# Mean squares by quarters of the tokens, and the root spread by a product, in a two-layer diffusion backbone

## The chip, the cores and the metric

The kernel runs on one core of a Trainium2 chip. The core has a matmul engine (TensorE, called PE in the profile; its loads of the stationary operand are shown apart as PEld), a vector engine (VectorE, DVE), a scalar engine with activation functions (ScalarE, ACT), a general engine (GpSimd, POOL) and a queue that issues transfers (SyncE, SP). Each engine works through its own instructions in order and waits on semaphores for the others. Matmuls write to PSUM, from where DVE and ACT read; everything else lies in SBUF, which has 128 partitions.

The metric is the device time of one execution in microseconds. It is given as the median of several runs. One further execution is profiled, and the rows quoted below are of that one.

## The reference, cut to what matters

There are 512 latent tokens and 256 context tokens of width 1024, all in f32. Layer 0 is grouped-query attention with a norm on every query and key head, layer 1 a bidirectional Mamba-2 mixer; each is followed by a gated FFN with a short convolution. Every one of these four sub-layers begins with an RMS norm over the 1024 features and an adaptive shift and scale:

```python
def rms_norm(x, g):
    xf = x.astype(jnp.float32)
    y = xf * lax.rsqrt(jnp.mean(xf * xf, axis=-1, keepdims=True) + EPS)
    return (y * g.astype(jnp.float32)).astype(x.dtype)

def modulate(x, shift, scale):
    return x * (1 + scale) + shift
...
    q_l = rms_norm(q_l.reshape(bsz, seq, N_HEADS, HEAD_DIM), q_norm)
    k_l = rms_norm(k_l.reshape(bsz, seq, N_KV_HEADS, HEAD_DIM), k_norm)
...
        y = rms_norm(y.reshape(bsz, length, D_INNER) * jax.nn.silu(z), norm_w) @ w_out
```

The norms are the subject here. The first kind takes the mean over 1024 features; the second, of queries and keys, over the 64 features of each head; the third, at the end of the Mamba mixer, over 2048.

## The kernel before

Activations lie transposed: features on the 128 partitions, tokens along the free axis, in eight tiles of 128 features. Weights are split into a high and a low part (`split`: ACT makes the high part, DVE or POOL the low part), and each product is three matmuls (`mm3`, the lines L105, L106 and L108 of the profile).

Since a token's features are spread over partitions, its sum of squares is a sum over partitions, and that is made on PE. `rstd_rows` does it for all norms. The squares are first added up over feature tiles, so one tile `sq` of 128 partitions by n tokens is left. Then:

1. For each 128 tokens a matmul has that piece of `sq` as stationary operand and a column of ones (for the heads: two columns, `g.blk`, one for each head of 64 features) as moving operand. The result (tile `ss...`, L236) has tokens on partitions and one or two columns.
2. DVE and ACT work the inverse root out on this small tile (128x2, 128x4 or 128x12; L239, L241, L243, L244): mean plus epsilon, logarithm, exponential of minus one half, one step of Newton's method. The last operation (L247) writes it out wide: 128 tokens by 128 equal columns (tile `rb...`).
3. After a pause PE transposes each wide piece (L253, tile `rsT...`), so that each of the 128 partitions holds the root for every token. For the segments of the sub-layer norms ACT copies the result to SBUF (`rs...`, L345).

The norms in the program: the first one over 512 latent tokens and one over the context (in `attention`, with the tiles named `a`); ten of query and key pairs (`normed`, named `q`, 768 tokens and two heads each); eight segments of 256 tokens in `Norm.gen` (named `f` for the FFNs, `s` for the Mamba mixer); and one over 512 tokens at the end of the mixer (named `y`). In `Norm.gen` the steps are spread over the steps of the product before, `lag` of them apart, and `modulated` then makes the input of the next product: DVE multiplies (L281), ACT adds the shift, DVE or POOL makes the low part.

The attention loop has eight pairs of heads with seven steps each. A step computes scores (`ps_s`), ACT takes the exponential (`pr`, L676), PE multiplies by the values (`ps_o`), DVE adds the sums (`acc`), and in between PE and DVE find the maxima for the next pair (`ps_m`, `ma`, `mb`). Behind each step `Fill.run` takes other work from a queue: the projections of later pairs (`ps_q`), their norms, products of the conditioning vector (`ps_ada`, transposed by `ps_adt`), later the output projection (`ps_d`). A generator in this queue that yields BREAK is left alone for three steps and costs the step's budget 1.0. The old head norm yields it three times: after the sums, and after each of two groups of transposes (512 and 256 tokens). The order within an engine is set by the program order with priorities by a scheduler when the program is built; the first part of attention is kept in written order.

In the profile some of these tiles carry the engine's read tile behind the arrow: `ssq<-cst,qsq` is the sum over heads, with the constants (`cst`) as moving and the squares (`qsq`) as stationary operand.

Of the kernel before, what the change touches and what calls it, by code (L numbers as in the profile page):

```python
# [7 lines left out]
P = 128  # L8
# [49 lines left out]
CST_IDENT, CST_BLK, CST_SEL, CST_COS, CST_SIN = 0, 128, 130, 132, 132 + L  # L58
NCST = 132 + 2 * L
# [167 lines left out]
def rstd_rows(g, sq, n, cols, width, name, bank):  # L227

    nc = g.nc
    c = cols.shape[-1]
    nt = n // P
    ps = bank(f"ss{name}")
    for t in range(nt):
        nc.tensor.matmul(ps[:, t * c : (t + 1) * c], sq[:, t * P : (t + 1) * P], cols, start=True, stop=True)  # L236
    small = lambda nm: g.p.tile([P, nt * c], F32, tag="rst", bufs=8, name=nm)
    a, y, u = small("rsa"), small("rsy"), small("rsu")
    nc.vector.tensor_scalar(a, ps[:, : nt * c], 1.0 / width, EPS, ALU.mult, ALU.add)  # L239
# [5 lines left out]
    rb = t3(g, f"rb{name}", n=n)  # L245
    wide = lambda v: v.unsqueeze(2).broadcast_to([P, nt * c, P // c])
    nc.vector.scalar_tensor_tensor(rb.rearrange("p (a b) -> p a b", b=P // c), wide(u), 1.5, wide(y), ALU.add, ALU.mult)  # L247
    yield BREAK
    out = []
    for t0 in range(0, nt, 4):  # L250
        pt = bank(f"rsT{name}")
        for t in range(t0, min(nt, t0 + 4)):
            nc.tensor.transpose(pt[:, (t - t0) * P : (t - t0 + 1) * P], rb[:, t * P : (t + 1) * P], g.ident)  # L253
        yield (pt, t0 * P, min(n, (t0 + 4) * P))
# [55 lines left out]
class Norm:  # L310
# [23 lines left out]
    def gen(self, seg, x, lag=2):  # L334

        i, a, b = seg
        g, nc, n = self.g, self.g.nc, b - a
# [7 lines left out]
        nc.scalar.copy(rs, next(rows)[0][:, :n])  # L345
# [33 lines left out]
def attention(g, fill, X, late):  # L379
# [41 lines left out]
    nc.sync.dma_start(g.cst, I["cst"][:, :CST_COS])  # L421
# [9 lines left out]
    def warmth(n):  # L431
        for _ in range(n):
            nc.tensor.matmul(warm[:, :P], g.ones, g.ones, start=True, stop=True)
# [8 lines left out]
    norm = rstd_rows(g, acc, L, g.ones[:, :1], D, "a", Bk)  # L442
# [12 lines left out]
    rsl, _, _ = next(norm)  # L455
# [12 lines left out]
    for m in range(KT):  # L468
# [11 lines left out]
        if m == 3:  # L480
            norm = rstd_rows(g, sqc, C, g.ones[:, :1], D, "a", Bk)
            next(norm)
        if m == 4:
            rsc = t3(g, "rsc", n=C)
            pt, _, _ = next(norm)
            nc.scalar.copy(rsc, pt[:, :C])
# [15 lines left out]
    man.__exit__(None, None, None)  # L502
    nc.sync.dma_start(g.cs, I["cst"][:, CST_COS:])
# [21 lines left out]
    def normed(qs, gain, eng):  # L525
# [51 lines left out]
    onesr = g.const.tile([P, P], F32R, name="onesr")  # L577
    nc.scalar.copy(onesr, g.ones)
# [5 lines left out]
    class Pair:  # L584
# [43 lines left out]
        def steps(self):  # L628
# [10 lines left out]
            def final(po, ps, acc, out):  # L639

                n = out.shape[-1]
                for e in range(2):
                    nc.tensor.matmul(ps[S64[e], :n], g.ones[:, :HD], acc[:, n * e : n * e + n], start=True, stop=True)
# [22 lines left out]
            for t in range(7):  # L666
                ps, pr = Sb("ps_s"), g.t3p.tile([P, 1024], F32, tag="pr", bufs=3, name="pr")
                for q0, n, k0, off in (((0, L, t * P, 0),) if t < 6 else ((L, C, L, 0), (L, C, L + P, C))):
# [5 lines left out]
                    for e in range(2):  # L674
                        nc.tensor.matmul(outs[e], onesr[S64[e]], self.diag[S64[e], q], start=False, stop=True)  # L675
# [203 lines left out]
def ssd(g, x, norm, wf, bg, close):  # L879
# [340 lines left out]
    norm = rstd_rows(g, acc[0], L, g.ones[:, :1], 2 * D, "y", lambda nm: Bank(g, nm))  # L1220
# [225 lines left out]
```

## Time and profile before

| | |
|---|---|
| median of 3 runs | 1912.97 us (1905.94 to 1915.4) |
| profiled execution | 1914.7 us, span of its instructions 1912.9 us |
| mean granted clock of PE | 0.994 |
| PE busy | 1876.5 us |
| DVE busy | 1311.2 us |
| ACT busy | 823.0 us |
| POOL busy | 309.8 us |

A row of a group names line, engine, operation, output and inputs, shape and count; then the busy time in all and the mean duration of one in ns; then the engine's idle time just before, with what ended it. Durations of matmuls overlap, since they are pipelined: what one occupies on PE is read from its start to the start of the next. A row of the time line gives start, duration, engine, line and tiles, and in brackets the idle time before.

### The profile page before, as it was taken

What the parts mean: (1) busy time and instruction counts of PE and PEld (TensorE: products, weight loads), DVE (VectorE), ACT (ScalarE), POOL (GpSimd) and SP (SyncE); (2) the same over time, 40 slices, a digit from 0 to 9 for tenths busy, and PEclk for the clock granted to TensorE, in tenths of its full rate; (3) what the DMA queues carried; (4) which work ended last, traced back from release to release, by engine and by line L of the source; (5) the groups of instructions that cost most, each with busy time, mean ns of one, the idle gap of its engine ahead of it and who ended that gap; (6) DMA issues with size and microseconds to landing.
All of it is one profiled execution on the core that took longest, in us unless ns stands there. A gap on an engine that the chain in (4) does not pass through costs nothing.

```text
span 1912.9 us, 27512 instructions
## 1 busy us (share of the span) xinstructions
PE 1876.5 (98%) x10834; PEld 1547.6 (81%) x10834; DVE 1311.2 (69%) x1943; ACT 823.0 (43%) x1426; POOL 309.8 (16%) x274
## 2 busy tenths in 40 slices
PE   9999999999999999999999999999999999999999
PEld 7866555678888888888888888888888878888887
DVE  5578778678877777444488777777888466565555
ACT  3634444255122222222266777776667352323331
POOL 2241111031000000000040344443434210000000
PEclk9989998999999999999999999999999999999999
DMA  9221332114434555221122443334443322323232
GB/s 337 78 89 45 113 112 95 34 45 166 132 122 132 174 188 166 66 67 60 62 89 87 121 118 115 126 113 133 120 138 115 91 77 86 102 88 110 88 100 88
DMA packets 73425, 210.02 MB, mean 110 GB/s; under 512 B 8912, under 2 KB 14416, under 8 KB 73168
## 3 DMA queue, kind: packets, MB, share of 16 engines
q1 hardware_dynamic: 73296, 208.26, 34.3%
q8 instruction: 85, 1.39, 0.3%
q14 instruction: 44, 0.36, 0.1%
HBM read 198.79 MB, written 6.82 MB: 107 GB/s over the span
## 4 chain that ended last, share of the span: by engine, by line
PE 79%; DVE 9%; issue 3%; ACT 2%; POOL 1%; DMA 1%; DVEq 0%; SPq 0%; POOLq 0%; ACTq 0%
PE ps_up L106 10%; PE ps_up L108 10%; PE ps_up L105 10%; PE ps_d L105 6%; PE ps_d L106 6%; PE ps_d L108 6%; PE ps_in L106 4%; PE ps_in L108 4%; PE ps_in L105 4%; PE ps_o L637 2%; PE ps_s L673 2%; PE ps_st L1033 2%; DVE ht L281 1%; PE ps_wo L108 1%; PE ps_wo L105 1%
## 5 line engine op out<-in xcount | busy, mean ns | idle before, releaser
L87 DVE TENSOR_TENSOR wl<-wst,wh 128x1024 fp32r<-128x1024 f32 x205 | 254.5, 1242 | 244.9 <-PE ps_up L106 137.7
L85 ACT CAST wh<-wst 128x1024 fp32r<-128x1024 f32 x211 | 221.2, 1049 | 423.2 <-DMA wst<-in_wup 333.8
L106 PE MATMUL ps_up<-hlf,wh 128*128 128x512 f32 x1008 | 357.0, 354 | 0.0
L105 PE MATMUL ps_up<-hhf,wh 128*128 128x512 f32 x1008 | 356.9, 354 | 0.0
L108 PE MATMUL ps_up<-hhf,wl 128*128 128x512 f32 x1008 | 356.8, 354 | 0.0
L105 PEld LDWEIGHTS ps_up<-hhf,wh 128*128 128x128 f32 x1008 | 190.5, 189 | 26.5
L106 PEld LDWEIGHTS ps_up<-hlf,wh 128*128 128x128 f32 x1008 | 190.6, 189 | 26.4
L108 PEld LDWEIGHTS ps_up<-hhf,wl 128*128 128x128 f32 x1008 | 190.5, 189 | 26.4
L105 PE MATMUL ps_in<-hhs,wh 128*128 128x512 f32 (+1 forms) x560 | 204.4, 365 | 0.0
L106 PE MATMUL ps_in<-hls,wh 128*128 128x512 f32 (+1 forms) x560 | 199.4, 356 | 0.0
L108 PE MATMUL ps_in<-hhs,wl 128*128 128x512 f32 (+1 forms) x560 | 198.7, 355 | 0.0
L105 PE MATMUL ps_d<-hdh,wh 128*128 128x512 f32 (+1 forms) x568 | 193.6, 343 | 1.4 <-DVE X L784 1.2
L108 PE MATMUL ps_d<-hdh,wl 128*128 128x512 f32 (+1 forms) x568 | 193.5, 341 | 0.0
L106 PE MATMUL ps_d<-hdl,wh 128*128 128x512 f32 (+1 forms) x568 | 193.0, 340 | 0.3 <-DVE hdl L87 0.3
L784 DVE SCALAR_TENSOR_TENSOR X<-ps_d,mod,X 128x512 f32<-128x512 f32 (+1 forms) x224 | 124.6, 583 | 36.9 <-PE ps_d L108 36.6
L106 PEld LDWEIGHTS ps_d<-hdl,wh 128*128 128x128 f32 x568 | 106.6, 188 | 14.8 <-DVE hdl L87 0.7
L105 PEld LDWEIGHTS ps_d<-hdh,wh 128*128 128x128 f32 x568 | 106.3, 188 | 14.8 <-DVE X L784 1.4
L105 PEld LDWEIGHTS ps_in<-hhs,wh 128*128 128x128 f32 x560 | 105.9, 189 | 15.1 <-issue 1.2
L108 PEld LDWEIGHTS ps_in<-hhs,wl 128*128 128x128 f32 x560 | 105.8, 189 | 14.8
L108 PEld LDWEIGHTS ps_d<-hdh,wl 128*128 128x128 f32 x568 | 106.7, 188 | 13.1
L106 PEld LDWEIGHTS ps_in<-hls,wh 128*128 128x128 f32 x560 | 106.0, 189 | 13.2
L676 ACT ACTIVATE pr<-ps_s 128x1024 f32<-128x1024 f32 x56 | 57.2, 1021 | 110.6 <-PE ps_s L675 109.6
(340 smaller groups left out, 3547.3 us busy)
## 6 DMA issues: line engine op xcount, KB each, us to landing
wst<-in_wup SPq DMA_DIRECT2D x88, 512.0 KB, 3.6
wada<-in_adaT SPq DMA_DIRECT2D x56, 512.0 KB, 3.9
wst<-in_win SPq DMA_DIRECT2D x48, 512.0 KB, 3.7
wst<-in_wdown SPq DMA_DIRECT2D x44, 512.0 KB, 3.6
E<-ad SPq DMA_DIRECT2D x64, 256.0 KB, 6.8
wada<-in_adaB SPq DMA_DIRECT2D x24, 512.0 KB, 4.6
ec<-ead SPq DMA_DIRECT2D x64, 128.0 KB, 5.0
wst<-in_wout SPq DMA_DIRECT2D x16, 512.0 KB, 3.6
```

Of the source, the lines that this page charges most:

```text
L85: keep(nc.scalar.copy(hi, src))
L87: keep(eng.tensor_tensor(lo, src, _r(hi), ALU.subtract))
L105: mm(out, wh, ah, start=first, stop=False)
L106: mm(out, wh, al, start=False, stop=False)
L108: mm(out, wl, ah, start=False, stop=last)
L281: nc.vector.scalar_tensor_tensor(t[:, c0:c1], ap, g.moda[layer][ca][:, m, v : v + 1], rs[:, c0:c1], ALU.mult, ALU.mult)
L637: nc.tensor.matmul(po[S64[e], :n], v, pr[:, 512 * e + off : 512 * e + off + n], start=first, stop=last)
L673: nc.tensor.matmul(outs[e], a[S64[e], k], b[S64[e], q], start=i == 0, stop=False)
L676: nc.scalar.activation(pr, ps, AF.Exp)
L784: nc.vector.scalar_tensor_tensor(ap, o[:, c0:c1], gate[:, m, v : v + 1], ap, ALU.mult, ALU.add)
L1033: nc.tensor.matmul(ps[:, d * 256 : (d + 1) * 256], Bt[:, t * P : (t + 1) * P], xw[d][t], start=t == ts[0], stop=t == ts[-1])
```

## The change

The sub-layer norm over a segment of 256 tokens (`rstd_all`) becomes one matmul with ones as the stationary operand and the squares as the moving one, 256 columns. Its result already has the sum on every partition, so nothing is transposed and nothing copied: the five operations of the root run on 128x256.

The norm over 512 tokens (`rstd_quarters`) takes four matmuls, one for each quarter of 128 tokens, with a stationary operand of 32 columns, so that each quarter's sums stand on 32 partitions of PSUM of their own (`sums_by_group`). The root is worked out on 128x128. Four products with a column of the identity, read 128 times, then bring each quarter to all partitions.

The head norm (`rstd_heads`) does the same with quarters of 192 tokens: within the 32 partitions 16 belong to each head. Four products with a pattern (`g.pick`), each over 64 partitions, spread the root; the two row halves write to two PSUM banks. DVE then multiplies twice 384 tokens, not 512 and 256. The generator yields BREAK twice, not three times.

The tile of ones is one column that is read with stride zero, also where scores take up the maxima (`onesr`) and where sums of exponentials are made. The constants grow by `blk` (32 columns) and `pick` (256 columns); they are loaded by a second transfer behind the first part of attention.

```diff
+def rsqrt_mean(g, ps, width, name):
     nc = g.nc
-    small = lambda nm: g.p.tile([P, nt * c], F32, tag="rst", bufs=8, name=nm)
-    a, y, u = small("rsa"), small("rsy"), small("rsu")
-    nc.vector.tensor_scalar(a, ps[:, : nt * c], 1.0 / width, EPS, ALU.mult, ALU.add)
+    n = ps.shape[-1]
+    w = t3(g, f"rs{name}", n=3 * n)
+    a, y, u = (w[:, i * n : (i + 1) * n] for i in range(3))
+    nc.vector.tensor_scalar(a, ps, 1.0 / width, EPS, ALU.mult, ALU.add)
     for f in ((lambda: nc.scalar.activation(y, a, AF.Ln)), (lambda: nc.scalar.activation(y, y, AF.Exp, scale=-0.5))):
         follow(g, f()) if g.tables else f()
     nc.vector.tensor_tensor(u, y, a, ALU.mult)
     nc.vector.scalar_tensor_tensor(u, y, -0.5, u, ALU.mult, ALU.mult)
-    rb = t3(g, f"rb{name}", n=n)
-    wide = lambda v: v.unsqueeze(2).broadcast_to([P, nt * c, P // c])
-    nc.vector.scalar_tensor_tensor(rb.rearrange("p (a b) -> p a b", b=P // c), wide(u), 1.5, wide(y), ALU.add, ALU.mult)
+    nc.vector.scalar_tensor_tensor(a, u, 1.5, y, ALU.add, ALU.mult)
+    return a
+
+def rstd_all(g, sq, width, name):
+    n = sq.shape[-1]
+    ps = Bank(g, f"ss{name}")[:, :n]
+    g.nc.tensor.matmul(ps, g.ones(P), sq, start=True, stop=True)
+    return rsqrt_mean(g, ps, width, name)
+
+def sums_by_group(g, sq, cols, name):
+    n = sq.shape[-1] // 4
+    ps = Bank(g, f"ss{name}")[:, :n]
+    for j in range(4):
+        g.nc.tensor.matmul(ps[32 * j : 32 * j + 32], cols, sq[:, j * n : (j + 1) * n], start=True, stop=True)
+    return ps
+
+def rstd_quarters(g, sq, width, name):
+    n = sq.shape[-1] // 4
+    r = rsqrt_mean(g, sums_by_group(g, sq, g.ones(32), name), width, name)
     yield BREAK
-    for t0 in range(0, nt, 4):
-        pt = bank(f"rsT{name}")
-        for t in range(t0, min(nt, t0 + 4)):
-            nc.tensor.transpose(pt[:, (t - t0) * P : (t - t0 + 1) * P], rb[:, t * P : (t + 1) * P], g.ident)
-        yield (pt, t0 * P, min(n, (t0 + 4) * P))
+    pt = Bank(g, f"rsT{name}")
+    for j in range(4):
+        g.nc.tensor.matmul(pt[:, j * n : (j + 1) * n], g.ident[:, 32 * j : 32 * j + 1].broadcast_to([P, P]), r,
+                           start=True, stop=True)
+    yield pt
+
+def rstd_heads(g, sq, name):
+    n = T // 4
+    r = rsqrt_mean(g, sums_by_group(g, sq, g.blk, name), HD, name)
+    yield BREAK
+    pt = [Bank(g, f"rsT{name}") for _ in range(2)]
+    for i in range(2):
+        for e in range(2):
+            rows = slice(64 * e, 64 * e + 64)
+            g.nc.tensor.matmul(pt[e][:, i * n : (i + 1) * n], g.pick[rows, i * P : (i + 1) * P], r[rows],
+                               start=True, stop=True)
+    yield [(pt[e], 2 * e * n, 2 * e * n + 2 * n) for e in range(2)]
...
-        for r in rstd_rows(g, sq, T, g.blk, HD, "q", Bk):
-            if r is not BREAK:
-                pt, c0, c1 = r
-                nc.vector.tensor_tensor(qs[:, c0:c1], qs[:, c0:c1], pt[:, : c1 - c0], ALU.mult)
-            yield BREAK
+        rows = rstd_heads(g, sq, "q")
+        yield next(rows)
+        for pt, c0, c1 in next(rows):
+            nc.vector.tensor_tensor(qs[:, c0:c1], qs[:, c0:c1], pt[:, : c1 - c0], ALU.mult)
+        yield BREAK
...
-        rows = rstd_rows(g, self.acc[seg, 6], n, g.ones[:, :1], D, self.name, lambda nm: Bank(g, nm))
-        next(rows)
+        rs = rstd_all(g, self.acc[seg, 6], D, self.name)
         for _ in range(lag):
             yield
-        rs = t3(g, f"rs{self.name}", n=n)
-        nc.scalar.copy(rs, next(rows)[0][:, :n])
```

Where instructions move, the built programs show it. PE in pair 0 of the attention loop, third step, before (each row: line, operation, output, moving and stationary tile, output shape, how many in a row):

```order
L236 MATMUL ssq<-cst,qsq 128x2 x6
L673 MATMUL ps_s<-qh,kh_967 128x512 x2
L673 MATMUL ps_s<-qh,kl_968 128x512 x2
L673 MATMUL ps_s<-ql,kh_967 128x512 x2
L675 MATMUL ps_s<-diag_1203,onesr 128x512 x2
L601 MATMUL ps_m<-kh_967,qh 128x256 x4
L637 MATMUL ps_o<-pr,v_744 64x512 x2
L253 MATMUL rsTq<-cst,rbq 128x128 x4
```

and the same place after:

```order
L259 MATMUL ssq<-qsq,cst 32x192 x4
L700 MATMUL ps_s<-qh,kh_912 128x512 x2
L700 MATMUL ps_s<-qh,kl_913 128x512 x2
L700 MATMUL ps_s<-ql,kh_912 128x512 x2
L702 MATMUL ps_s<-diag_1171,onesr 128x512 x2
L628 MATMUL ps_m<-kh_912,qh 128x256 x4
L664 MATMUL ps_o<-pr,v_733 64x512 x2
L286 MATMUL rsTq<-rsq,cst 128x192 x4
```

Six sums of two columns became four of 192 columns on 32 partitions each, and four transposes (two more follow a few steps later) became four products of 192 columns.

PE in pair 5, before, second step, with filling from the queue behind `ps_o`:

```order
L637 MATMUL ps_o<-pr,v_742 64x512 x2
L128 MATMUL ps_ada<-wada,sc_83 32x512 x8
L673 MATMUL ps_s<-qh,kh_1988 128x512 x2
L673 MATMUL ps_s<-qh,kl_1989 128x512 x2
L673 MATMUL ps_s<-ql,kh_1988 128x512 x2
L675 MATMUL ps_s<-diag_2673,onesr 128x512 x2
L601 MATMUL ps_m<-kh_1994,qh 128x512 x2
L637 MATMUL ps_o<-pr,v_743 64x512 x2
L236 MATMUL ssq<-cst,qsq 128x2 x6
```

and a later step of pair 5 after, where the queue has nothing left:

```order
L664 MATMUL ps_o<-pr,v_733 64x512 x2
L700 MATMUL ps_s<-qh,kh_1814 128x512 x2
L700 MATMUL ps_s<-qh,kl_1815 128x512 x2
L700 MATMUL ps_s<-ql,kh_1814 128x512 x2
L702 MATMUL ps_s<-diag_2667,onesr 128x512 x2
L664 MATMUL ps_o<-pr,v_734 64x512
L628 MATMUL ps_m<-kh_1820,qh 128x512 x2
L664 MATMUL ps_o<-pr,v_734 64x512
```

The three `ps_ada` products of pair 5 and its `ssq` stand in pair 4 now, and between the products of scores and values nothing stands in the last four steps.

DVE at the end of attention, the norm of the second segment of 256 tokens, before:

```order
L239 TENSOR_SCALAR rsa<-ssf_4110 128x2
L784 SCALAR_TENSOR_TENSOR X<-ps_d_4123,mod_88,X 128x256
L243 TENSOR_TENSOR rsu<-rsy,rsa 128x2
L244 SCALAR_TENSOR_TENSOR rsu<-rsy,rsu 128x2
L784 SCALAR_TENSOR_TENSOR X<-ps_d_4137,mod_88,X 128x256
L247 SCALAR_TENSOR_TENSOR rbf_4121<-rsu,rsy 128x256
L281 SCALAR_TENSOR_TENSOR ht<-X,moda_99,rsf_4151 128x256
```

and after:

```order
L234 TENSOR_SCALAR rsf_4022<-ssf_4020 128x256
L811 SCALAR_TENSOR_TENSOR X<-ps_d_4043,mod_88,X 128x256
L238 TENSOR_TENSOR rsf_4022<-rsf_4022 128x256
L811 SCALAR_TENSOR_TENSOR X<-ps_d_4061,mod_88,X 128x256
L239 SCALAR_TENSOR_TENSOR rsf_4022<-rsf_4022 128x256
L240 SCALAR_TENSOR_TENSOR rsf_4022<-rsf_4022 128x256
L811 SCALAR_TENSOR_TENSOR X<-ps_d_4080,mod_88,X 128x256
L88 TENSOR_TENSOR wl<-wst,wh 128x1024
L315 SCALAR_TENSOR_TENSOR ht<-X,moda_99,rsf_4022 128x256 x3
```

All four operations of the root are 256 columns wide now, one more eviction (`X<-ps_d`) and a weight split stand ahead of the first modulation, and no wait for PE's transposes lies between.

More of the change, by code (lines that the diff above doesn't have):

```diff
@@ L432, in warmth @@
         for _ in range(n):
[L433 removed]
+            nc.tensor.matmul(warm[:, :P], g.ones(P), g.ones(P), start=True, stop=True)
     warmth(38)
@@ L454, in attention @@
     warmth(5)
-    rsl, _, _ = next(norm)
+    rsl = next(norm)
     next(mods[0])
@@ L480, in attention @@
         if m == 3:
[L481 to L486, printed above, removed]
+            rsc = rstd_all(g, sqc, D, "a")
         for j in range(6):
```

47 lines of the change are left out of this document (23 added, 24 removed).

## The prediction

> **What bounds the kernel now.** I read the page's busy shares and clock row first, then the waits of PE, then the time line around the norms.
>
> ```profile
> PE 1876.5 (98%) x10834; PEld 1547.6 (81%) x10834; DVE 1311.2 (69%) x1943; ACT 823.0 (43%) x1426; POOL 309.8 (16%) x274
> PEclk9989998999999999999999999999999999999999
> DMA  9221332114434555221122443334443322323232
> ...
> PE rsTq L253 <- DVE rbq L247: 2.9, 2, 1.8
> PE rsTs L253 <- DVE rbs L247: 1.3, 2, 1.0
> PE rsTf L253 <- DVE rbf L247: 1.2, 2, 1.0
> ```
>
> PE is busy in 98% of the span and idle for 36.4 us. So the time is PE's work, plus its waits, plus what a lowered clock adds. The rows below the dots (waits of PE: total, times, longest) show that the transposes of the old norm are among PE's longer waits: 5.4 us in all. The clock row has digits under 9 only in the first 335 us.
>
> The sums and the transposes of the ten query and key norms (lines L236 and L253), as groups:
>
> ```profile
> L236 PE MATMUL ssq<-cst,qsq 128*128 128x2 f32 x120 | 15.8, 259 | 0.3 <-ACT qsq L528 0.3
> L253 PE MATMUL rsTq<-cst,rbq 128*128 128x128 f32 x60 | 10.3, 286 | 2.9 <-DVE rbq L247 2.9
> ```
>
> A f32 matmul is two instructions, so 120 rows are 60 matmuls, six for each of ten norms. Most of these run between the steps of the attention loop (120 to 390 us). What they occupy there is read as start to next start:
>
> ```profile
> 221.00 0.40 PE L673 MATMUL ps_s<-qh,kl 64*128 64x512 f32 x2
> 221.23 0.41 PE L673 MATMUL ps_s<-ql,kh 64*128 64x512 f32 x2
> ...
> 221.69 0.42 PE L601 MATMUL ps_m<-kh,qh 64*128 64x512 f32 x2
> 222.04 1.08 PE L637 MATMUL ps_o<-pr,v 128*64 128x512 f32 x4
> 223.05 0.66 PE L253 MATMUL rsTq<-cst,rbq 128*128 128x128 f32 x4
> 223.46 0.36 PE L105 MATMUL ps_q<-hha,wh 128*128 128x256 f32 x1
> ...
> 283.51 1.92 PE L128 MATMUL ps_ada<-wada,sc 128*32 128x512 f32 x16
> 285.37 0.50 PE L673 MATMUL ps_s<-qh,kh 64*128 64x512 f32 x2
> ...
> 287.74 1.50 PE L236 MATMUL ssq<-cst,qsq 128*128 128x2 f32 x12
> 289.17 0.50 PE L673 MATMUL ps_s<-qh,kh 64*128 64x512 f32 x2
> ```
>
> Twelve ssq instructions take 1.43 us (287.74 to 289.17) although they stream two columns each: their 128x128 weight loads set the pace. Four transposes take 0.41 us, the other two half of that, 0.20. One norm costs PE 2.04 us.
>
> **The change, part by part.** *Sums by quarters (ten norms).* Four f32 matmuls of 192 columns into four column groups. The nearest row is ps_ada, which has the same form (128*32, groups 0 to 3 in turn): 8 matmuls of 512 columns in 1.86 us. By columns that is 1.86 x 4/8 x 192/512 = 0.35 us; with about 0.1 for entering another array shape (ps_m to ps_o takes 0.35 where the ps_s pair before takes 0.23) I take 0.47. Bounds: 0.35, and 1.43 if the groups ran in turn. *The product that spreads the root.* Four f32 matmuls of 64 rows and 192 columns, in pairs on the two row halves and into two banks. The trace shows that ps_s pairs on row halves overlap: two of 512 columns in 0.23 us. It has no f32 pair on row halves; the f32 pair on column halves (ps_o, four instructions, 1.01 us) scales to 1.01 x 192/512 = 0.38, twice is 0.76, plus a little: 0.79. Bounds: 0.7, and 1.6 without overlap. One norm then costs 1.26 instead of 2.04; ten give **-7.8 us** (bounds -10 and +10).
>
> A rule that speaks against this: the Trainium skill, TensorEngine Tiling (Array Packing), section Key Properties, says that a change of the tiling mode drains the engine. The 0.12 us between ps_m and ps_o agrees with it. With two more such changes for each norm the ten would give about 2.4 us less.
>
> *The chain between them, on DVE and ACT.* Rows of the old four operations by form, and the nearest rows for 192 and 256 columns:
>
> ```profile
> L239 DVE TENSOR_SCALAR rsa<-ssq 128x12 f32<-128x12 f32 x10 | 1.7, 165 | 11.2 <-PE ssq L236 11.0
> L243 DVE TENSOR_TENSOR rsu<-rsy,rsa 128x12 f32<-128x12 f32 x10 | 7.0, 702 | 2.9 <-ACT rsy L241 2.9
> L244 DVE SCALAR_TENSOR_TENSOR rsu<-rsy,rsu 128x12 f32<-128x12 f32 x10 | 2.7, 271 | 0.3
> L247 DVE SCALAR_TENSOR_TENSOR rbq<-rsu,rsy 128x768 f32<-128x768 f32 x10 | 11.7, 1173 | 0.4
> L247 DVE SCALAR_TENSOR_TENSOR rbf<-rsu,rsy 128x256 f32<-128x256 f32 x5 | 2.2, 443 | 0.2
> L1157 DVE TENSOR_TENSOR dw<-ps_end,acsT x2: 347/352/356, 1042.9 to 1043.2; 128x192 f32<-128x192 f32 x2
> L1144 PEld LDWEIGHTS ps_end<-acsT,cst x4: 185/189/190, 1035.0 to 1035.4; 128*128 128x128 f32 x4
> ```
>
> Old: 0.17 + 0.70 + 0.27 + 1.17 = 2.31 us of DVE. New: four of 192 columns at 0.35 = 1.4. The two ACT operations grow by perhaps 0.1 each. The chain from the sums to the multiplied tile shortens by 0.8 on DVE and about as much on PE. (The last row, a column of the identity read with stride zero as weights, shows 189 ns, like any load; so the single column that replaces the ones costs nothing.) Before the loop, PE waits for this chain:
>
> ```profile
> 79.67 0.66 PE L253 MATMUL rsTq<-cst,rbq 128*128 128x128 f32 x4 [1.08 <-DVE rbq L247]
> 93.84 0.50 PE L601 MATMUL ps_m<-kh,qh 64*128 64x256 f32 x4 [1.01 <-ACT qh L85]
> ```
>
> I take **-2** for these (bounds 0 and -4).
>
> *The clock.* Three times the granted clock falls to half, each time right behind ssq:
>
> ```profile
> 95.14 1.75 PE L236 MATMUL ssq<-cst,qsq 128*128 128x2 f32 x12
> 122.99 2.24 PE L236 MATMUL ssq<-cst,qsq 128*128 128x2 f32 x12 [0.34 <-ACT qsq L528]
> ...
> 96.00:98.00 2.00, 2.00 (x12) 2.00 (x12) 1.19 (x3) 0.00 (x0) 0.00 (x0) 0.56 0.29 70
> 124.00:128.00 4.00, 4.00 (x18) 1.72 (x22) 3.90 (x8) 1.84 (x5) 0.30 (x1) 0.50 0.60 178
> 292.00:296.00 4.00, 4.00 (x16) 2.39 (x13) 3.44 (x7) 2.27 (x4) 1.19 (x1) 0.50 0.44 168
> 296.00:300.00 4.00, 4.00 (x18) 2.90 (x20) 1.14 (x4) 0.76 (x1) 0.00 (x0) 0.50 0.00 0
> ```
>
> (Columns of the last four: window, its length, busy times of the five engines' parts, clock, DMA share, GB/s.) By ends of the stretched matmuls the drops last about 3.5, 6.8 and 10.2 us, which loses half of 20.5, about 10 us. Twelve matmuls that stream two columns leave the array almost empty for 1.5 us; with a short wait beside them that seems to be enough. The new sums take a third of that and stream 192 columns. I take half: **-5** (bounds -10 and +5, if a new wait makes a new drop).
>
> *The eight 256-token segments* (ends of attention, both FFNs' inputs, SSD's input): four ssf instructions and two transposes become one matmul of 256 columns; the ACT copy goes.
>
> ```profile
> 408.08 0.50 PE L236 MATMUL ssf<-ones,sqf 128*128 128x1 f32 x4
> 408.44 0.36 PE L105 MATMUL ps_d<-hhol,wh 128*128 128x256 f32 x1
> ...
> 423.36 0.44 PE L253 MATMUL rsTf<-cst,rbf 128*128 128x128 f32 x2 [1.01 <-DVE rbf L247]
> ...
> L1033 PE MATMUL ps_st<-xw,Bt 128*128 128x256 f32 x160 | 37.2, 379 | 0.0
> L345 ACT COPY rsf<-rsTf 128x256 f32<-128x256 f32 x5 | 1.8, 368 | 7.5 <-PE rsTf L253 7.5
> ```
>
> PE: 0.36 + 0.2 before, 2 x 37.2/160 = 0.46 after, -0.1 each; and the waits for rbf and rbs, 2.5 us, lose their place. But DVE gets four operations of 256 columns (4 x 0.44) for 1.1 us, +0.65 each, and the two ACT operations grow by what the copy gives back, so the chain to the first modulated tile is as long as it was and part of the wait comes back at ps_first. I take **-2** (bounds -4 and +3).
>
> *The two whole-row norms (start, SSD's end).* The start stands behind transfers (the first digit of the DMA row), and at SSD's end eight matmul tiles lie between sums and product. Eight weight loads fewer, eight f32 passes more: **0**. The second constant transfer is 147 KB, queued on SP ahead of the cosines and long before the first sum needs it: **0**.
>
> *The order.* A norm now takes two turns of the fill queue, not three, so query projections and adaLN products come earlier, and pair 5 is left without filling. Pair lengths before (pairs 5 and 4):
>
> ```profile
> 274.68:311.94 37.26, 35.82 (x220) 18.42 (x220) 29.45 (x46) 15.45 (x21) 5.66 (x3) 0.86 0.40 141
> 243.98:274.68 30.70, 30.63 (x198) 18.70 (x194) 22.10 (x33) 12.27 (x18) 5.43 (x3) 1.00 0.24 84
> ```
>
> Of pair 5's 35.8 us of busy PE, 5 are half clock, 5.6 are three ps_ada products that move ahead (3 x 1.86) and about 1.2 the norm's saving and its moved sum: 24 remain. Of DVE's 29.5 about 6 leave (three copies of the products, two weight splits at 1.2, the norm's 0.9): 23.5 remain. Neither covers the other, and each step hands over from one to the other, so PE will stand idle there a little more: **+2** (bounds 0 and +6).
>
> Sum: -7.8 - 2 - 5 - 2 + 2 = -14.8 us on the profiled execution's 1914.7 us, so 1899.9. The median of the runs is 1912.97, 1.7 lower; that gives 1898, and I say **1899**.
>
> **Rivals.** *The clock holds.* If ssq was the sole cause of all three drops, the term is -10, not -5, and pair 5 shortens without a new drop: 1890 to 1893. For it: each drop follows an ssq. Against it: other ssq had no drop behind them, and the eight-column ps_adt products at 293 stay. The Trainium skill, TensorE: Matmul & The Clock Gate, section Part 1, describes a half rate after an idle window of about 3.4 us; the lengths 3.5, 6.8 and 10.2 agree as one, two and three windows.
>
> *Nothing gained.* DVE sets the loop's pace in truth (22 to 29 us in pairs of 30 to 37), or the f32 pairs on row halves don't overlap: the -7.8 shrinks to 0, the clock stays, and only the chain before the loop and the segments help: about 1909, within 0.5%. For it: bursts in which DVE has no gap. Against it: PE is busy in 30.63 of 30.70 us in pair 4.
>
> *Slower.* Pair 5, now without filling, waits on DVE at every step, and the clock falls at its start and stays at half through it into the projections behind it. Then 24 us of matmuls cost 24 more, and 10 us of ps_d another 10; less the 5 that pair 5 loses now, less the 5 of the two earlier drops, less 9.8 for the other terms, this is +14 and ends near 1927. It decides from about 30 us of matmuls at half clock on. Against it: pair 4 holds a clock of 1.00 although DVE is busy there for 22 of 31 us.
>
> **How the numbers follow.** About 0.5% (9.6 us) is what a measurement of this kernel tells from no change. Forecast with its half clock term: 0.50 (own range 1893 to 1904); clock holds: 0.17; nothing gained: 0.25; slower: 0.08. Faster 0.67, same 0.25, slower 0.08. The range 1886 to 1912 takes in the first three down to their ends and leaves out the slow case and a little at each side.
>
> **What would show it.** Right: ssq groups with an array of 128*32 and under 0.5 us from their start to the next row; rsTq about 0.8; no wait of PE on rb; full clock at 96 and 124 us; pair 5 near 27 us. Wrong: rsTq at 1.3 or more (no overlap), a clock of 0.5 anywhere from 270 to 330 us, or waits of PE on DVE in pair 5 of more than 6 us.

## The result, and the profile after

The changed kernel takes 1923.95 us (median of 8 runs, 1920.82 to 1931.26), the kernel before 1910.96 us in the runs beside it. The ratio is 1.0083 (95% interval 1.0069 to 1.0097): slower by 13 us by the medians, where 14 us of gain were forecast. The profiled execution has a span of 1924.4 us against 1912.9. Three of the later runs had one execution at a much lower granted clock (2046 to 3068 us); it is left out of their times and ratios.

The page of the changed kernel, busy times and clock row:

```profile
PE 1873.9 (97%) x10786; PEld 1541.0 (80%) x10786; DVE 1332.2 (69%) x1943; ACT 827.2 (43%) x1417; POOL 291.7 (15%) x274
...
PEclk9999989999999999999999999999999999999999
```

PE works 2.6 us less than before and stands idle for 50.5 us instead of 36.4. So the question is what PE waits for now. Its waits over the whole run of the changed kernel (total, times, longest):

```profile
PE ps_xt L1034 <- DVE ec L1127: 8.4, 6, 2.5
PE ps_first L106 <- ACT hhf L324: 4.4, 3, 2.4
PE ps_adt L135 <- DVE ada_sb L131: 3.4, 2, 2.1
...
PE ps_s L702 <- DVE diag L651: 3.2, 3, 2.3
PE ps_xt L1034 <- DVE xf L1137: 2.9, 1, 2.9
PE rsTq L286 <- DVE rsq L240: 2.8, 3, 1.6
...
PE rsTq L286 <- DVE raw L566: 2.0, 1, 2.0
```

The largest new wait is at `ps_xt`. That is the Mamba mixer, where the change touches no line: the mixer works through eight groups of heads, and `ps_xt` is the first product of a group that needs PSUM banks which the group before still holds (DVE empties them with `ec`, L1127). Taking the start of `ps_cb` as the mark of a group, the seven periods between the eight marks are, kernel before first, then the changed one (window, its length, busy times, granted clock; rows two and three, and the sum):

```profile
1102.31:1157.37 55.06, 54.82 (x328) 47.57 (x327) 40.27 (x47) 38.08 (x83) 21.58 (x20) 1.00 0.40 117
1157.37:1212.43 55.06, 54.82 (x327) 47.54 (x326) 41.17 (x48) 38.04 (x83) 22.26 (x20) 1.00 0.39 112
...
sum 385.71, PE 383.81 PEld 332.93 DVE 289.39 ACT 267.76 POOL 152.88; mean PE 54.83 PEld 47.56 DVE 41.34 ACT 38.25 POOL 21.84
```

```profile
1105.99:1161.90 55.91, 54.79 (x328) 47.61 (x327) 41.99 (x47) 37.27 (x81) 20.70 (x19) 1.00 0.37 113
1161.90:1220.81 58.91, 56.36 (x327) 48.53 (x326) 43.78 (x48) 39.17 (x83) 19.45 (x19) 0.97 0.34 108
...
sum 398.73, PE 387.10 PEld 335.02 DVE 299.21 ACT 268.23 POOL 140.98; mean PE 55.30 PEld 47.86 DVE 42.74 ACT 38.32 POOL 20.14
```

398.7 less 385.7 is 13.0 us: the difference of the spans is 11.5, so all of it and a little more arises here. Of the 13.0 us, 9.7 are idle time of PE (length less busy time, 11.6 against 1.9) and 3.3 are PE's busy time, which grows in the two longest groups, where the granted clock is 0.97. Up to the first mark the changed kernel is 1.0 us ahead (1046.67 against 1047.70). Why PE waits at `ps_xt` is seen on SP's queue. Its time line around one group, kernel before and then changed:

```profile
1138.42 13.36 SPq L95 DMA_DIRECT2D wst<-in_win  x3
1151.82 5.29 SPq L1065 DMA_DIRECT2D E<-ad  x8
```

```profile
1136.85 25.56 SPq L96 DMA_DIRECT2D wst<-in_win  x4
1162.47 5.40 SPq L1092 DMA_DIRECT2D E<-ad  x8
```

The eight `E` transfers feed work on POOL, ACT and DVE. `ec` does not read `E`, but in the order of POOL and DVE the steps that lead to it stand behind this work. Before, the transfers leave 5.5 us ahead of the mark (1151.82 against 1157.37) and the first step of this work on POOL starts 0.9 us ahead of it; now they leave 0.6 us behind it (1162.47 against 1161.90), and the first step starts 4.9 us behind. They stand on SP behind weight transfers (`wst`), and these now wait for something else. Waits of SP from 1009 to 1446 us, before and then changed:

```profile
SPq L95 <- DVE wl L87: 189.6, 29, 14.8
SPq L95 <- PE ps_in L108: 83.4, 13, 8.2
```

```profile
SPq L96 <- PE ps_in L109: 224.6, 32, 14.0
SPq L96 <- PE ps_yo L1125: 43.2, 6, 8.3
SPq L96 <- DVE wl L88: 35.4, 5, 9.5
```

The staging tile `wst` and the split weights `wh` and `wl` share ten buffers, which the scheduler hands out when the program is built. Before, a staging tile mostly got the buffer of an older staging tile, free as soon as DVE has split it. Now it mostly gets the buffer of an older weight, free only when PE is done with it.

### The profile page after: what moved, and what is told of

The parts are those of the page before. It is cut to its first block, busy times and chain, and to the rows that moved or that the text cites. A ratio compares the mean times of both kernels' runs of the same rounds, so it can differ in the third digit from the quotient of the medians.

```text
span 1924.4 us, 27479 instructions
## 1 busy us (share of the span) xinstructions
PE 1873.9 (97%) x10786; PEld 1541.0 (80%) x10786; DVE 1332.2 (69%) x1943; ACT 827.2 (43%) x1417; POOL 291.7 (15%) x274
## 4 chain that ended last, share of the span: by engine, by line
PE 70%; DVE 13%; issue 5%; ACT 2%; POOL 2%; DMA 2%; SPq 0%; POOLq 0%; DVEq 0%; ACTq 0%
PE ps_up L107 10%; PE ps_up L106 10%; PE ps_up L109 10%; PE ps_d L106 6%; PE ps_d L107 6%; PE ps_d L109 6%; DVE xf L990 3%; PE ps_o L664 2%; PE ps_in L109 2%; PE ps_in L107 2%; PE ps_in L106 2%; PE ps_s L700 2%; DVE wl L88 1%; DVE Bf L990 1%; PE ps_wo L106 1%
## 5 line engine op out<-in xcount | busy, mean ns | idle before, releaser
L107 PEld LDWEIGHTS ps_d<-hdl,wh 128*128 128x128 f32 x568 | 106.7, 188 | 14.8 <-DVE hdl L88 0.7
L107 PEld LDWEIGHTS ps_in<-hls,wh 128*128 128x128 f32 x560 | 106.6, 190 | 13.5
```

What stands on the lines that cost most here:

```text
L107: mm(out, wh, al, start=False, stop=False)
```

## The experiments

Each run was compared with the kernel before on the same chip; ratios have their 95% interval. Of the rows not quoted, periods and stage lengths are read from time lines and windows as above.

**Which part of the change brings the late transfers.** The build alone shows that only the new route at the mixer's input norm (the three segments named `s`) gives the mixer's staging tiles other buffers. So it was undone alone, and done alone.

```diff
+        if self.name == "s":      # r1: old route (sums, transposes, ACT copy) for s only
+            rows = rstd_rows(...)
+        else:
         rs = rstd_all(g, self.acc[seg, 6], D, self.name)
```

> The changed kernel with one part undone: the three segment norms at the SSD's input (name s) go by the old route (four ssf instructions of one column, chain of narrow operations, two transposes, ACT copy); heads, quarters and the other segments stay new. Theory 1 (staging buffers): the new route at this one norm only shifts which of the ten weight buffers the scheduler gives to the staging tiles (wst) in the SSD stage; there they then wait for PE to finish with an older weight instead of for DVE's split, SP's queue holds the E transfers behind them, and PE waits at ps_xt in each group. Then this run's first waits of SP at the wst transfers are again on DVE wl, the period of ps_cb is 55.1 us again (after: 55.9 to 59.3), and the time is 13 us under the changed kernel's 1924: 1911, ratio to before 0.998 to 1.000. Rival 2 (the norms' own work: wider operations on DVE, lowered clock in the attention stage): no more than 1 us comes back, 1922 to 1924, ratio 1.006 to 1.008, and the SSD period stays at 55.9 and more.

Measured: 1.0019 (1.0011 to 1.0028), 1911.52 us; periods of 55.05 to 55.9, 387.0 us in all; the largest of SP's waits is on DVE again:

```profile
SPq L96 <- DVE wl L88: 194.6, 30, 14.8
SPq L96 <- PE ps_in L109: 80.4, 13, 8.2
```

The second run is the mirror: the kernel before, with `rstd_all` for `s` and nothing else.

> The kernel before with one part done: only the three segment norms at the SSD's input take the new route (one product with ones, root on 128x256). Theory 1 (staging buffers): these three norms alone bring the whole loss: SSD periods of 56 to 59 us, PE waits at ps_xt of some 11 us, time 1911 + 12 to 14 = 1923 to 1925, ratio 1.006 to 1.0075. Rival 2 (the loss comes from many norms' work and the clock): three segments change nothing, 1910 to 1912, ratio 0.999 to 1.001.

Measured: 1.0085 (1.0069 to 1.0101), 1922.9 us; periods of 56.5 to 58.6, 402.8 us in all. PE's first waits in the run of r2:

```profile
PE ps_xt L1036 <- DVE ec L1129: 11.3, 6, 2.2
PE ps_first L106 <- POOL hlf L313: 3.1, 6, 1.0
```

Theory 1 holds on both sides, and the rival falls: three segments bring the loss, in the groups of the mixer and not where they run. r1 keeps 0.2%, more than theory 1 allowed; that remainder is taken up under *Context and start*.

**Is it the time of the E transfers?** In r5 the whole change stays, and the issue of `E` moves one step up in the program. r6 does the same to the kernel before.

```diff
+        eb = []
+        for r in range(4):
+            for d in range(2):
+                row = d * 32 + 4 * gi + r
+                eb.append(t2("E"))
+                nc.sync.dma_start(eb[-1], ad[row : row + 1, :].broadcast_to([P, L]))
         yield
         Bt = t3(g, "Bt")
...
-                e = t2("E")
-                nc.sync.dma_start(e, ad[row : row + 1, :].broadcast_to([P, L]))
+                e = eb[2 * r + d]
```

> The whole changed kernel, with one edit in the SSD stage: the eight broadcast transfers of a group into the E tiles are issued one step earlier in the program, so that on SP they stand two weight transfers earlier. Theory 1 (SP's queue: E stands behind a staging transfer that waits for PE, and comes some 6 us late): with E early, PE waits at ps_xt under 3 us in all, the period is 55.2 us or less although the staging tiles still get the buffers of the changed kernel; time 13 us under the changed kernel, 1909 to 1912, ratio 1.000 to 1.002. Rival 2 (the late split of the weights on DVE, not the late E, makes PE wait): periods stay at 56 to 59 us, 1920 to 1924.

> The kernel before with the same early E transfers. Theory 1: E is in time there already (5.5 us ahead of ps_cb) and PE waits only 1.9 us at ps_xt, so 0 to -2 us: 1906 to 1909, ratio 0.999 to 1.000. The difference to r5_after_early_E is then the price of the rest of the change: 2 to 4 us by r1_after_old_s. Rival 2: no relation; the SSD period moves by more than 1 us either way.

Measured: r5 1.0022 (1.0012 to 1.0032), r6 1.0007 (0.9998 to 1.0016). In r5 PE's waits in the mixer's groups are gone; the only one left from 1005 to 1446 us lies ahead of them:

```profile
PE ps_end L1176 <- DVE acsT L1171: 1.4, 1, 1.4
```

The groups take 383.7 us in r5 and 384.0 in r6, 2 us less than in the kernel before. But r5 does not keep the buffers of the changed kernel, as its expectation supposed: moving `E` made the scheduler deal them out anew. SP's waits from 1005 to 1446 us, in r5 and then in r6:

```profile
SPq L96 <- DVE wl L88: 217.3, 26, 20.8
SPq L96 <- PE ps_in L109: 53.6, 16, 8.7
```

```profile
SPq L95 <- PE ps_in L108: 199.7, 26, 10.8
SPq L95 <- DVE wl L87: 81.2, 15, 10.4
```

So r5 alone does not separate the buffers from the time of `E`. r6 does: its staging tiles wait mostly for PE, as in the changed kernel, yet with `E` early the groups are short. Both runs pay about 5 us elsewhere: from the last mark to the end of the span they take 484.0 and 484.6 us, the kernel before 479.5. There is a new wait there, 2.4 us of `ps_wo` on `hly`, but the idle time of the 120 us behind the mark is much as before (5.1 and 6.0 us, before 5.4); 4.7 us of lowered clock are new in both. r15 (below) has the same wait and no lowered clock behind it, so this price is not paid in every execution.

r3 and r4 tried another cure: a tag of its own for the staging tile, 3 buffers for it and 7 for the weights.

```diff
-    st = t4(g, "wst")
+    st = g.p.tile([P, 1024], F32, tag="t4s", bufs=3, name="wst")
```

> The whole changed kernel, with the staging tile wst in a tag of its own (3 buffers) and wh and wl in the other 7 of the ten, so that a staging transfer can only wait for the split of an older staging tile. Theory 1: the SSD period is 55.1 us or less whatever the norms do, E transfers are issued some 5 us ahead of ps_cb as in the kernel before, PE waits at ps_xt under 3 us in all; time 1911 or less (the FFNs could move too, since their staging tiles waited on PE in both kernels): 1900 to 1912. Rival 2: SSD is no better, 1920 to 1926.

> The kernel before with the same split of the ten weight buffers (3 staging, 7 weights). Theory 1: SSD as in the kernel before (55.1 us for each group), and against r3_after_stage this shows what the new norms are worth without the accident of the buffers: r3 is 0 to 4 us faster than this run (the traces have the changed kernel 1 us ahead at the start of the SSD stage). Rival 2: r3 is slower than this run by some 10 us.

Measured: r3 1.0215 (1.0201 to 1.0228), r4 1.0229 (1.0216 to 1.0243). I was wrong: `E` comes even later, from the second group on, and the mixer takes 408 and 411 us. (The rest of their loss, 9 us of each profile, lies ahead of the mixer and behind it and was not traced.) But these misses complete the picture: here the staging tiles wait for DVE alone, `E` is late all the same, and the groups are long. Over all kernels the length of a group goes with the time at which its `E` transfers are issued:

| kernel | E issued, relative to the mark | period that follows |
|---|---|---|
| r5, r6, r13, r15 (below) | 14 to 22.7 us ahead | 54.6 to 55.0 us |
| before, r1, r7 to r12, r14, r16 (below) | 1.4 to 6.4 us ahead | 54.6 to 55.9 us |
| r3, r4, first group | 4.2 us ahead | 54.8, 54.9 us |
| changed, r2 | 0.0 to 0.6 us behind | 55.9 to 59.3 us |
| r3, r4, other groups | 1.7 to 2.7 us behind | 57.7 to 60.5 us |

So late and early are told apart by `E`, whatever frees the staging tiles. How long a late group becomes is not: at the same 0.6 us behind the mark the changed kernel has periods of 55.9 and of 59.3 us. DVE's instructions stand in another order in these groups, since the scheduler orders the engines anew with every edit; what sets the size of the loss was not settled.

**Where the gain of the head norms went.** r7 has the ten head norms new and all other norms old; r8 adds a turn, as the old norm had it.

```diff
-            nc.vector.tensor_tensor(qs[:, c0:c1], qs[:, c0:c1], pt[:, : c1 - c0], ALU.mult)
-        yield BREAK
+            nc.vector.tensor_tensor(qs[:, c0:c1], qs[:, c0:c1], pt[:, : c1 - c0], ALU.mult)
+            yield BREAK      # r8
```

> The changed kernel with all parts undone but the ten head norms (sums by quarters in column groups, product with the pattern, two turns): segments, the context norm, start and SSD's end go by the old route; the SSD stage has the weight buffers of the kernel before. Theory A (the gain on PE, some 6 to 8 us, is eaten by new waits of PE on DVE in pairs 0, 4 and 5 and before the loop, and by the clock drops that they set off): 1907 to 1911, ratio 0.999 to 1.0015; idle time of PE from 60 us to the first ps_up some 5 us above the kernel before. Theory B (the forecast: the heads gain all of their PE time and the drops go): 1898 to 1902, ratio 0.995 to 0.997. Theory C (the 3 to 4 us that r1_after_old_s lost come from the start, the context or the f0 and f1 segments): then this run is 3 us or more faster than r1_after_old_s.

> As r7_heads_only, and a norm takes three turns of the fill queue again, as in the kernel before (the two halves are multiplied in turns of their own). Theory A1 (the new waits in pairs 0, 4 and 5 come from the order: two turns, both multiplications at once, pair 5 without filling): the waits go and it is 3 to 6 us faster than r7_heads_only: 1902 to 1906. Theory A2 (the waits come from the root's four operations of 192 columns on DVE, wherever they stand): within 2 us of r7_heads_only.

Measured: r7 0.9991 (0.9981 to 1.0), r8 1.0013 (1.0003 to 1.0022). Theory A of r7 holds in its waits; its clock drops are weighed further down. Theory C holds beside it, since r7 lies 0.3% below r1. From 60 us to the first `ps_up`, three profiles of code that is the same there (before, r2, r6) and five with the new heads give, as length = PE's own work at full clock + idle + lost by lowered clock (at 60 us all eight are within 2 us of the same place: their first `ps_c` starts at 61.7 to 63.7 us):

| | length | own work | idle | clock |
|---|---|---|---|---|
| before, r2, r6 | 388.8, 381.5, 380.1 | 364.4, 363.0, 362.9 | 14.3, 13.5, 13.9 | 10.2, 5.0, 3.4 |
| r7 | 380.8 | 356.0 | 19.9 | 4.8 |
| r8 | 382.1 | 355.7 | 23.4 | 3.1 |
| r9 (below) | 369.0 | 353.2 | 15.8 | 0.0 |
| r12 (below) | 376.5 | 353.4 | 21.6 | 1.6 |
| changed kernel | 388.1 | 355.0 | 18.3 | 14.8 |

The split is rough: r7 and r9 run the same matmuls and differ by 2.8 us in own work. PE saves some 7 us of work and waits some 6 us longer, and the turns of the queue are not the reason (r8 waits more, so A1 falls). Two rows of the changed kernel show what DVE does in pair 0:

```profile
133.05 2.24 POOL L560 TENSOR_TENSOR raw<-raw,cs 128x512 f32<-128x512 f32 x1
...
134.09 1.41 DVE L239 SCALAR_TENSOR_TENSOR rsq<-rsq 128x192 f32<-128x192 f32 x1
...
136.02 0.98 PE L286 MATMUL rsTq<-rsq,cst 64*128 64x192 f32 x6 [2.00 <-DVE raw L566]
```

One operation of the root takes 1.41 us instead of 0.35, until POOL's operation beside it is over, and PE's next product waits 2.00 us for a bank. Behind it the clock falls to 0.59 and 0.55 (136 to 144 us). That points to the root's operations on DVE, so r9 leaves three of the four out, and r12 moves them to POOL.

```diff
+    if not refine:           # r9, head norms: no Newton step
+        return y
     nc.vector.tensor_tensor(u, y, a, ALU.mult)
     nc.vector.scalar_tensor_tensor(u, y, -0.5, u, ALU.mult, ALU.mult)
     nc.vector.scalar_tensor_tensor(a, u, 1.5, y, ALU.add, ALU.mult)
```

> As r7_heads_only, but the head norms leave out the refinement of the root (the last three of its four DVE operations on 128x192, so the product takes exp of -0.5 ln directly; the kernel computes slightly other query and key norms). The rows have 2.0 us of DVE for a root, of which 1.67 go, 16.7 us in ten norms. Theory D (the root's wide operations on DVE are what PE waits for): idle time of PE from 60 us on falls from 19.9 to about 14, as in the kernel before, and the time to 1902 to 1905, 4 us or more under r7_heads_only. Theory O (the waits come from the order: weight splits and bank releases that moved into pairs 0 and 4): idle stays at 18 or more, within 2 us of r7_heads_only, 1907 to 1909.

> As r7_heads_only, with the refinement of the head norms' root on POOL (four operations of 192 columns there, each some 0.5 us by POOL's 1.3 us for 512) instead of three on DVE. Theory D1 (DVE's occupancy is what costs, as r9_heads_no_refine suggests): DVE loses the same 16.7 us, and the time comes most of the way to r9: 1896 to 1901. Theory D2 (the length of the root's chain costs: the product comes too late, whoever computes it): the chain becomes longer, 1908 to 1913. Theory D3 (POOL beside DVE stretches DVE's operations, as rows of 2.3 us for 1.22 show beside POOL's rotation): in between, 1903 to 1907.

Measured: r9 0.9942 (0.9925 to 0.996), 1896.08 us; r12 0.9994 (0.9979 to 1.0009). PE's first waits in r9 and in r12:

```profile
PE ps_s L742 <- DVE diag L691: 3.7, 2, 2.3
PE ps_first L107 <- POOL hlf L354: 2.9, 5, 1.0
```

```profile
PE rsTq L322 <- POOL rsq L272: 5.7, 3, 3.7
PE ps_s L746 <- DVE diag L695: 3.4, 2, 2.0
```

DVE is busy for 15.8 us less in r9 than in r7 (1295.6 against 1311.4), the time falls by 9 us, and no wait at `rsTq` is left. r12 relieves DVE by nearly as much, but the root comes later (POOL's four operations take 0.60 to 0.92 us each), and PE waits for it. Before the loop (60 us to the first step) r9 takes 53.7 us, r7 57.0, r12 59.4, with 1.9, 5.6 and 6.4 us of idle PE: there the length of the chain counts (theory D2). In pairs 0 to 6 r9 takes 223.9, r12 225.4, r7 229.8, but PE's idle time is no less in r9 and r12 (8.1 and 9.3 us) than in r7 (7.1). 3.2 us of r7's length are the lowered clock of pair 0, which r9 and r12 do not have; the rest is in PE's busy time and stays open. So theory D1 (DVE's occupancy within the loop) is not shown by waits. The waits at `diag` in pair 4 stay in all three, so that part is order, as theory O had it.

r14 asks whether the old route had this cost too: it leaves the two narrow operations out of the kernel before.

> The kernel before, with the refinement left out in its ten head norms (two narrow DVE operations, 0.97 us a norm, 9.7 us in all; the wide one stays and spreads exp of -0.5 ln as it is). Theory N (any relief of DVE in the head norms is worth about 0.6 us of time for 1 us of DVE, as r9 had 9.4 for 16.7): 1903 to 1905, ratio 0.997 to 0.998. Theory W (the old route doesn't make PE wait, so its narrow operations cost nothing; what cost time were the new route's wide ones): 1907 to 1909, ratio 0.999 to 1.001.

Measured: 1.0002 (0.999 to 1.0014). Theory W: there the refinement costs nothing that is seen. (DVE's relief was smaller than planned, 6.8 us, since the wide operation in its other form took 1.46 us, not 1.17.)

**Context and start.** r10 adds the context norm to r7, r11 the start norm.

> As r7_heads_only, with the context norm (256 tokens, at 37 us) new as well. Theory 3 (of the 5 us by which r1_after_old_s lies above r7_heads_only, this norm brings most: its root puts 3.2 us of DVE ahead of the ada_sb copy, PE waits 2.05 us at ps_adt at 42.5 us, and a half clock follows): 3 to 5 us slower than r7_heads_only, 1912 to 1914, the wait at ps_adt back. Rival: within 1 us of r7_heads_only; then start, f0 or f1 bring it.

> As r7_heads_only, with the start norm (512 tokens by quarters) new as well. Theory 3: nothing, since the start waits for transfers: within 1 us of r7_heads_only. Rival: 3 us or more slower.

Measured: r10 1.0026 (1.0017 to 1.0035), r11 0.9994 (0.9981 to 1.0006). The start costs nothing; the context norm costs 0.35%, some 7 us (4 to 9 by the intervals), which is also what r1 had left. Its place in the changed kernel, at 40 us:

```profile
39.77 0.42 DVE L239 SCALAR_TENSOR_TENSOR rsa<-rsa 128x256 f32<-128x256 f32 x1
40.08 1.81 POOL L88 TENSOR_TENSOR wsl<-wst,wsh 128x768 fp32r<-128x768 f32 x1 [6.78 <-ACT wsh L86]
40.23 1.94 DVE L240 SCALAR_TENSOR_TENSOR rsa<-rsa 128x256 f32<-128x256 f32 x1
42.09 0.41 DVE L131 COPY ada_sb<-ps_ada 128x256 f32<-128x256 f32 x1
...
42.56 0.61 PE L135 MATMUL ps_adt<-cst,ada_sb 128*128 128x2 f32 x4 [2.05 <-DVE ada_sb L131]
```

Four operations of the root stand on DVE ahead of the copy that PE needs, and the last one takes 1.94 us instead of 0.42, because POOL's split runs beside it. PE waits 2.05 us; in r10 it is 2.04, and there the clock falls behind it (0.66 at 44 to 48 us; in the changed kernel's profile it stays at 1.00). From 40 to 52 us r10 has 2.0 us of idle PE and 1.7 us of lowered clock, r7 none of either. That is 3.7 us; where the rest of the 0.35% lies was not found.

**Do the causes add up?** r13 is the whole change with the context norm old, `E` early and the heads' refinement on POOL. r15 and r16 are the whole change without the refinement in any norm, with `E` early and as it was.

> The whole change with what the runs point to: the context norm by the old route, the E transfers of the SSD stage one step earlier, the head norms' refinement on POOL; heads, start, segments and SSD's end new. If the three causes add up: r12_heads_refine_pool and 0 to 2 us less for the segments and the early E (r5 lay 0.7 us, r6 1.3 us above what they started from or repaired, so no more than that): 1895 to 1901 under theory D1, 1908 or more under D2. If the causes hide each other, more than 4 us above r12.

> The whole changed kernel with the refinement of the root left out in every norm (three DVE operations fewer for each) and the E transfers of the SSD stage one step earlier. If what cost time was the root's wide operations on DVE and the late E, and nothing else of the change: r9_heads_no_refine (1896) less 0 to 3 us, since the context norm's 1.7 us of DVE ahead of ada_sb and the segments' wide operations go too: 1893 to 1897, ratio 0.992 to 0.995. If segments and context cost by something else (their product with ones, the place of the bank), 1900 to 1904.

> The same without the early E transfers. The scheduler gives the staging tiles of the SSD stage a third assignment of the ten weight buffers here (of three loads that stood ahead of E in the changed kernel, some wait for the split and some for PE). Theory 1 says that the SSD period follows from when E is issued and from nothing else: E issued 5 us or more ahead of ps_cb gives 55.1 us and a time within 2 us of r15; E behind ps_cb gives 56 to 59 us and 6 to 13 us more than r15. Rival: the period was long because of the segment norm's own work ahead of the stage; then it is 55 here, whenever E comes.

Measured: r13 1.0008 (0.9995 to 1.002), 2 to 3 us above r12, between the two expectations. r15 0.988 (0.9862 to 0.9897) and r16 0.9884 (0.9866 to 0.9902): faster than both kernels by more than 20 us, and faster than either expectation of r15 had it; what brings the surplus was not traced. In r16 the scheduler deals the ten buffers out in yet another way; `E` leaves 5.6 to 6.4 us ahead of the mark, and the periods are 54.7 to 55.7 us. Theory 1 and the rival of r16 both forecast that, so r16 does not decide between them. r5 and r13 do: there the segment norm has all its operations, `E` is early, and the periods are 54.6 to 55.0 us. What r15 and r16 leave out is real work; r14 shows that leaving it out of the old head norms is worth nothing that can be measured, so there the gain needs the new route.

## Why the prediction was wrong, point by point

- **The failed step is the eight 256-token segments (-2, bounds -4 and +3).** I priced the operations and the waits around them, and under *The order* I followed only the queue of the attention loop. The three segments at the mixer's input cost 12 us there (changed kernel against r1: 1.0083 against 1.0019) and 16 us alone (r2), by dealing out the weight buffers of the next stage anew. No term and no rival of mine allowed for that; the build of the changed kernel would have shown that SP's weight transfers wait for other engines.
- **The context norm** has 256 tokens too, but it is not one of the eight, and no term of mine holds it. It costs some 7 us, of which 3.7 are traced to its place ahead of `ada_sb` on DVE. For the eight I had priced such a chain (1.1 us more of DVE), but not who queues behind it.
- **The head norms, -7.8: right in size on PE, and without effect.** Sums take 0.46 us from start to next start (forecast 0.47), the product 0.62, or 0.85 where `ps_q` follows (forecast 0.79): rows of the changed kernel,

```profile
127.58 0.53 PE L259 MATMUL ssq<-qsq,cst 128*32 128x192 f32 x8
128.04 0.50 PE L700 MATMUL ps_s<-qh,kh 64*128 64x512 f32 x2
...
130.41 0.92 PE L286 MATMUL rsTq<-rsq,cst 64*128 64x192 f32 x8
131.03 0.53 PE L700 MATMUL ps_s<-qh,kh 64*128 64x512 f32 x2
```

  and PE's own work falls by 7 us. The array packing rule's 2.4 us less are not seen: the array changes its shape and the sums still take 0.46. But the loop gives 6 us back as waits. The rival *nothing gained* came nearest ("DVE sets the loop's pace in truth"): its price, about 1909, is what r7 and r8 show (1909.0, 1911.4), though r9 and r12 leave open whether DVE's occupancy is the reason.
- **The chain on DVE, 1.4 us instead of 2.31: mis-sized.** Measured per norm:

```profile
L238 DVE TENSOR_TENSOR rsq<-rsq 128x192 f32<-128x192 f32 x10 | 5.9, 585 | 3.9 <-ACT rsq L236 3.8
L239 DVE SCALAR_TENSOR_TENSOR rsq<-rsq 128x192 f32<-128x192 f32 x10 | 5.8, 577 | 0.1
L240 DVE SCALAR_TENSOR_TENSOR rsq<-rsq 128x192 f32<-128x192 f32 x10 | 5.1, 509 | 0.2
L234 DVE TENSOR_SCALAR rsq<-ssq 128x192 f32<-128x192 f32 x10 | 3.5, 351 | 10.6 <-PE ssq L259 10.6
```

  0.585 + 0.577 + 0.509 + 0.351 = 2.02 us: on average only the one that reads PSUM keeps to 0.35. The medians of all four are 0.35 to 0.36; a few of the other three are stretched to 1.3 to 1.5 us beside POOL. I had set an undisturbed row against the old operations' means, which have stretched ones in them. r9 shows that leaving three of the new ones out gains 9 us, r14 that leaving out two of the old ones gains none. Before the loop the number -2 came out for the heads by luck (r7: 57.0 us from 60 us on, code of before 58.2 to 59.7): PE's idle time there rose from 4.5 to 4.6 us to 5.6, and what fell was lowered clock, from 1.7 us to none.
- **The clock, -5: wrong.** The drops at 96 and 124 us, behind the old sums, are gone as forecast. A new one stands at 136 to 144 us in most profiles with the new heads. And the 10 us that I read from one profile were a high draw: the same code lost 3.4 to 10.2 us. The mean granted clock over all executions is 0.995 in r7 and 0.995 in the kernel before beside it, so the heads' term is nothing. Nor is `ssq` the only cause: the profile before has a fourth drop, at 34 to 38 us (0.70 and 0.50), behind a wait of 1.31 us and ahead of any head norm. The changed kernel's drop from 278 to 294 us, one of my signs of "wrong", is absent in r5, which has the same code there. That term could not be read from one execution.
- **Order and pair 5, +2: sign right, place wrong.** Without lowered clock pair 5 takes 30.6 us in r5 and r7 (forecast 27, code of before 31.8 in r2 and r6), and the idle time rose in pairs 0 and 4 rather than there.
- **Start and constants, 0: right** (r11 against r7: 0.9994 against 0.9991).

## What to carry to other kernels

Where a scheduler hands out buffers and order, a small edit can change a stage that it does not touch: compare the built programs far behind the edit as well, above all which engine frees the buffers that the transfers on an in-order queue wait for. A cheaper product on PE is worth little where PE waits for the chain on DVE that leads to it; price what stands behind a DVE operation, not only the operation. And read a term that depends on the granted clock from several executions, not from one.

## What was not expected of the hardware

- DVE operations with two SBUF inputs wait until a POOL operation beside them ends: 0.42 became 1.94 us, 0.35 became 1.41, in the rows above. The Trainium skill, SBUF — State Buffer, section Who interferes with whom, says that a DVE instruction with two SBUF inputs contends with a GpSimd instruction that reads SBUF, and calls the shared port pair an exclusive lock. The trace agrees: the DVE row at 40.23 ends 0.28 us behind POOL's end at 41.89. The old route had this too: in the profile before, a product of 128x12 took 2.09 us at 122.2 us, beside a split on POOL that ended at 124.3, where others of its kind took 0.16.
- Waits of PE of only 2.0 us had half clock behind them (at 136.0 us in the changed kernel, at 44.2 us in r10); the wait of 2.05 us at 42.6 us in the changed kernel had none. The Trainium skill, TensorE: Matmul & The Clock Gate, Part 1, names an idle window of about 3.4 us; by that, such a short wait should not do it alone. What of the sparse work beside it counts was not settled here.
- Why the scheduler deals the buffers out differently after the new segment norm was not found out; only that it does, and what follows from it.
